# Weight parts at 32 places in turn, and the first layer's SwiGLU in three 256-column matmuls per weight tile

## The chip, the cores and the metric

The kernel runs on one core of a Trainium2 chip. A core has a matrix engine (TensorE, PE in the profile; its weight loads are listed apart as PEld), a vector engine (VectorE, DVE), a scalar engine (ScalarE, ACT), GpSimd (POOL) and a queue engine (SyncE, SP) that issues transfers. They share an on-chip memory of 128 partitions (SBUF); TensorE writes its results into banks of a second one (PSUM), from which the vector and scalar engines read. Each engine has its own instruction stream, and the streams wait for one another through semaphores.

The metric is the device time of one execution, in microseconds; lower is better.

## What is computed

Two layers of a decoder trunk over 256 positions and 1024 channels, in float32. The parts that matter here, cut from the reference:

```python
D_MODEL, SEQ, DEPTH, D_FF = 1024, 256, 2, 2816

def swiglu(h, w_in, w_out):
    a, b = jnp.split(h @ w_in, 2, axis=-1)
    return (jax.nn.silu(a) * b) @ w_out

for l in range(DEPTH):
    x = x + 0.5 * swiglu(rmsnorm(x, ffn1_norm[l]), ffn1_w_in[l], ffn1_w_out[l])
    h = rmsnorm(x, mix_norm[l])
    hq, hf, hi, hg, aq, ak, av, ga, gb = jnp.split(h @ w_in[l], split_idx, axis=-1)
    ...   # a gated recurrence and a dilated attention, merged by two gates
    x = x + merged @ w_out[l]
    x = x + 0.5 * swiglu(rmsnorm(x, ffn2_norm[l]), ffn2_w_in[l], ffn2_w_out[l])
```

All weights are read once, some 250 MB, and every product is a matrix of 256 positions against a weight matrix.

## The kernel before, in words

**Split operands.** A float32 product is made of three products of type float32r. Each operand is split in two parts: `hi`, the value rounded to that type, and `lo`, the rest. The product is hi·hi + hi·lo + lo·hi. Weights are split on the chip: `unit` (L200 on) starts a transfer of up to 1024 x 256 weights into a tile `raw` on SP's queue, then takes two `weight_parts` tiles of 4 x 128 rows each; ACT copies `raw` into `hi` (L211), DVE subtracts to get `lo` (L212). `raw` has three buffers and the tile of the parts, `wp`, four. The activations are kept split as well, feature-major: `xp` (the normed input of a stage), `hp` (the hidden values of a SwiGLU), `pp` and `obp` (in the mixer).

**Where the parts lie.** `weight_parts(at, c)` (L96) makes a tile of 8,704 bytes per partition, and puts `hi` at byte `at` and `lo` 4,096 bytes behind it; 512 bytes are spare. `unit` asks for `at` = 0 and `wide` for 32. In the program as built, the four `wp` tiles begin at bytes 83,680, 92,384, 101,088 and 109,792 of the partition, all 96 past a multiple of 128. So the parts of `unit` begin 96 past a multiple of 128 and those of `wide` on a multiple of 128. `xp`, `hp`, `pp` and `obp` all begin on multiples of 128.

**Three ways to multiply.** A weight tile here is 128 rows by 128 columns.

- `mm_pair` (L230 on) takes two matmuls for one: `hi` weights against both activation parts side by side, 512 columns (L237), and `lo` weights against the activation's `hi` part, 256 columns (L238), added into the second half of the same bank. Each block of 128 outputs has a bank of its own, and its two halves are added afterwards by `total` (L267): ACT copies one half out (L269), DVE adds the other (L270).
- `mm_feat` (L216 on) takes three matmuls of 256 columns (L226, L227, L228), all into the same 256 columns of a bank. Two blocks of 128 outputs share one bank and nothing is added afterwards.
- `wide` (L272 on, matmuls at L247 to L249) turns it round: the activations are the stationary side, and `wp` is streamed, 512 columns at a time, three matmuls each.

Each matmul loads its stationary operand itself, so there are as many weight loads as matmuls.

**Stages.** For each layer: a SwiGLU (`ffn`, L335 on), the mixer (`mix`), a second SwiGLU. A SwiGLU first runs over 11 blocks of 256 hidden columns; a block takes two units, `pa` and `pb`, each summed by `total`, multiplied by the norm's scale `Rb2` (L351, L356), passed through Silu, multiplied, and split into `hp`. Then it runs over four blocks of 256 outputs, each from three units over the 22 blocks of hidden rows, and adds half of the result into `xT` (L389, four instructions a block). All SwiGLU products use `mm_pair`, but for the last output product of the second layer, which uses `wide`. The mixer uses `mm_feat` (through `full`) and `wide`.

PSUM has eight banks: four for these products (`ps_mm`), three for small ones, one for transposes. A planner orders the instructions of each engine when the program is built.

Of the kernel before, what the change touches and what calls it, by code (L numbers as in the profile page):

```python
# [1 line left out]

# [1 line left out]

# [5 lines left out]
F32 = mybir.dt.float32  # L10
# [3 lines left out]
OP = mybir.AluOpType  # L14
# [5 lines left out]
DFF = 2816  # L20
KF = DFF // 128
CU = 256
# [5 lines left out]
FIRST = 2  # L28
# [49 lines left out]
def trunk(ctx, tc, x, ffn1_norm, ffn1_w_in, ffn1_w_out, mix_norm, w_in, lb_logits, out_norm,  # L78
          q_norm, k_norm, w_a, w_b, w_out, ffn2_norm, ffn2_w_in, ffn2_w_out, ctab, out):
    nc = tc.nc  # L80
# [4 lines left out]
    ps_mm = ctx.enter_context(tc.tile_pool(name="ps_mm", bufs=MM, space=PSUM))  # L85
    ps_sm = ctx.enter_context(tc.tile_pool(name="ps_sm", bufs=SM, space=PSUM))

    def bank(tag="sm"):
        return ps_sm.tile([128, 512], F32, name=tag, tag=tag, bufs=SM if tag == "sm" else 8 - MM - SM)

    def parts_of(pool, n, name, at=STEP, pad=STEP):

        t = pool.tile([128, n * 2 * T + pad // 4], F32R, name=name, bufs=1)
        return t[:, at // 4:at // 4 + n * 2 * T].rearrange("p (k a t) -> p k a t", a=2, t=T)

    def weight_parts(at, c):  # L96


        n = KH * CU
        t = wts.tile([128, 2 * n + LINE // 4], F32R, name="wp", bufs=WB)  # L100
        return [t[:, at // 4 + i * n:at // 4 + (i + 1) * n].rearrange("p (k c) -> p k c", c=c) for i in range(2)]

    def halves(p):
        return p[:, :, 0, :], p[:, :, 1, :]


    xT = const.tile([128, KD, T], F32, name="xT")
    xp = parts_of(const, KD, "xp", 128, LINE)
    xh, xl = halves(xp)
    ct = const.tile([128, C_END], F32, name="ct")  # L110
# [89 lines left out]
    def unit(w, r0, nk, col, step=0):  # L200
        raw = wts.tile([128, KD, CU], F32, name="raw", bufs=RB)
        for a in range(0, nk, step or nk):
            n = min(step or nk, nk - a)
            nc.sync.dma_start(raw[:, a:a + n, :], w[r0 + a * 128:r0 + (a + n) * 128, col:col + CU].rearrange(
                "(k p) c -> p k c", p=128))
        parts = []
        for a in range(0, nk, step or KH):
            n = min(step or KH, nk - a)
            hi, lo = weight_parts(0, CU)
            r = raw[:, a:a + n, :]  # L210
            nc.scalar.activation(hi[:, :n, :], r, AF.Copy)  # L211
            nc.vector.tensor_sub(lo[:, :n, :], r, hi[:, :n, :].bitcast(F32))  # L212
            parts += [(hi[:, k, :], lo[:, k, :]) for k in range(n)]
        return parts
# [15 lines left out]
    def mm_pair(ps, wu, ap, k0, nk, first, last):  # L230

        for k in range(nk):
            hi, lo = wu[k]
            s, e = first and k == 0, last and k == nk - 1
            for fb in range(2):
                f = slice(fb * 128, (fb + 1) * 128)
                nc.tensor.matmul(ps[fb], hi[:, f], ap[:, k0 + k], start=s, stop=False, skip_group_check=True)  # L237
                nc.tensor.matmul(ps[fb][:, 1, :], lo[:, f], ap[:, k0 + k, 0, :], start=False, stop=e,  # L238
                                 skip_group_check=True)
# [17 lines left out]
    def bank_pair():  # L257
        return [ps_mm.tile([128, 2, T], F32, name="mm") for _ in range(2)]

    def full_pair(w, col, ap, step=0):  # L260

        wu = unit(w, 0, KD, col, step)
        ps = bank_pair()
        mm_pair(ps, wu, ap, 0, KD, True, True)
        return ps

    def total(dst, ps):  # L267
        for fb in range(2):
            nc.scalar.activation(dst[:, fb, :], ps[fb][:, 1, :], AF.Copy)  # L269
            nc.vector.tensor_add(dst[:, fb, :], ps[fb][:, 0, :], dst[:, fb, :])  # L270
# [20 lines left out]
    def v2(a):  # L291
        return a.rearrange("p (a b) -> p a b", a=2)


    def norm_parts(gi, l):
        for k in range(KD):
            nc.scalar.activation(xh[:, k, :], xT[:, k, :], AF.Copy, scale=gain(gi, l, k))
            nc.vector.scalar_tensor_tensor(xl[:, k, :], xT[:, k, :], gain(gi, l, k),  # L298
                                           xh[:, k, :].bitcast(F32), op0=OP.mult, op1=OP.subtract)
# [16 lines left out]
    def square_sums_x(work, x0):  # L316
        ss = work.tile([128, 2], F32, name="nss", bufs=1)
        sq = work.tile([128, 4, D // 4], F32, name="nsx", bufs=1)
        for h in range(2):
            nc.scalar.activation(sq, x0[:, :, h, :], AF.Square, accum_out=ss[:, h:h + 1])  # L320
        return ss

    def norm_scale(work, ss):
        ms = work.tile([128, 2], F32, name="nms", bufs=1)
        nc.vector.tensor_scalar(ms, ss, 1.0 / D, EPS, op0=OP.mult, op1=OP.add)
        nc.gpsimd.tensor_tensor(rstd, ms, mhalf[:, 0:2], op=OP.pow)
        pr = bank("tr")
        for h in range(2):
            nc.tensor.transpose(pr[:, h * 128:(h + 1) * 128], rstd[:, h:h + 1].to_broadcast([128, 128]), ident)
        nc.vector.tensor_copy(Rb, pr[:, :T])  # L330

    Rb2 = Rb[:, None, :].to_broadcast([128, 2, T])


    def ffn(l, gi, w1, w2, to_out, x0=None):  # L335
        norm_parts(gi, l)
        with ExitStack() as es:
            fp = es.enter_context(tc.tile_pool(name="ffn", bufs=2))
            hp = parts_of(fp, KF, "hp")
            hh, hl = halves(hp)  # L340
            xt = None
            for j in range(DFF // CU):
                pa = full_pair(w1, j * CU, xp, step=0 if j or l or gi else FIRST)
                if j == 0:
                    with tc.tile_pool(name="norm", bufs=2) as work:
                        norm_scale(work, square_sums(work) if x0 is None else square_sums_x(work, x0))
                if j == 1 and l == 0 and gi == 0:
                    load_tables()
                a = fp.tile([128, 2, T], F32, name="fa")
                total(a, pa)  # L350
                nc.vector.tensor_mul(a, a, Rb2)  # L351
                nc.scalar.activation(a, a, AF.Silu)
                pb = full_pair(w1, DFF + j * CU, xp)
                b = fp.tile([128, 2, T], F32, name="fb")
                total(b, pb)
                nc.vector.tensor_mul(b, b, Rb2)  # L356
                nc.vector.tensor_mul(a, a, b)
                s = slice(2 * j, 2 * j + 2)
                nc.scalar.activation(hh[:, s, :], a, AF.Copy)
                nc.vector.tensor_sub(hl[:, s, :], a, hh[:, s, :].bitcast(F32))  # L360
            if to_out:
                xt = fp.tile([128, 2, D], F32, name="xt", bufs=1)
                for h in range(2):
                    for q in range(2):
                        p = bank()
                        for j in range(4):
                            nc.tensor.transpose(p[:, j * 128:(j + 1) * 128],
                                                xT[:, 4 * q + j, h * 128:(h + 1) * 128], ident)
                        nc.vector.tensor_copy(xt[:, h, q * 512:(q + 1) * 512], p)
            if to_out:  # L370
                for c in range(D // CW):
                    ps = wide(w2, c * CW, hp, KF)
                    for h in range(2):
                        y = fp.tile([128, CW], F32, name="fy", bufs=2)
                        nc.vector.scalar_tensor_tensor(y, ps[h], 0.5, xt[:, h, c * CW:(c + 1) * CW],
                                                       op0=OP.mult, op1=OP.add)
                        nc.sync.dma_start(out[0, h * 128:(h + 1) * 128, c * CW:(c + 1) * CW], y)
            else:
                for c in range(D // CU):
                    ps = bank_pair()  # L380
                    k0 = 0
                    for nk in (8, 8, 6):
                        wu = unit(w2, k0 * 128, nk, c * CU)
                        mm_pair(ps, wu, hp, k0, nk, k0 == 0, k0 + nk == KF)
                        k0 += nk
                    for fb in range(2):
                        xs = xT[:, 2 * c + fb, :]
                        for a in range(2):
                            nc.vector.scalar_tensor_tensor(xs, ps[fb][:, a, :], 0.5, xs, op0=OP.mult, op1=OP.add)  # L389
# [387 lines left out]
```

## Time and profile before

| what | value |
|---|---|
| median of two runs | 1431.3 us (1431.08 and 1431.51) |
| the profiled execution, its own time | 1430.89 us |
| its span, first to last instruction | 1428.8 us |
| DVE busy, whole span | 1059.1 us (74%) |
| ACT busy, whole span | 842.7 us (59%) |
| POOL busy, whole span | 93.1 us (7%) |
| transfers | 252.95 MB, mean 177 GB/s, the main queue's packets 54.1% of the 16 engines' span |
| matmuls, weight loads | 9,426 each |

The span is the time between the first and the last instruction of the program; 2.1 us of the execution lie around it. The profile has one line for each engine with its busy time, the span in 40 slices, the chain of work that ended last, and groups of instructions by line and operation. Matmuls are pipelined, so the duration of one (some 280 or 390 ns) says little. What says how fast TensorE goes is the distance from one start to the next, which the timeline or the first and last start of a group give.

### The profile page before, as it was taken

The page shows a single profiled execution, that of the slowest core. Times are in us where ns is not written, and L with a number is a line of the kernel's source. Part 1 is how long each engine was busy: PE and PEld are TensorE (multiplying, and loading weights), DVE is VectorE, ACT ScalarE, POOL GpSimd, SP SyncE. Part 2 cuts the span into 40 slices and gives each one's busy share as a digit, 9 for nine tenths or more (in the row PEclk, how much of TensorE's full clock was granted, in tenths as well). Part 3 has the DMA queues.
Part 4 walks back from the last instruction along what each step waited for, and adds up shares of the span by engine and source line. Part 5 has one row for each costly group of instructions (what it writes and reads, how often), then busy time and mean ns, then how long its engine had stood idle before and what let it go on. Part 6 is the DMA issues. An engine that isn't in the chain of part 4 may idle for free.

```text
span 1428.8 us, 23520 instructions
## 1 busy us (share of the span) xinstructions
PE 1419.3 (99%) x9426; PEld 1267.5 (89%) x9426; DVE 1059.1 (74%) x1664; ACT 842.7 (59%) x1435; POOL 93.1 (7%) x86
## 2 busy tenths in 40 slices
PE   8999999999999999999999999999999999999998
PEld 7888898998889998888888888988988899988887
DVE  6877569876976587786577866798779766787763
ACT  6655447657864566565455554666577646565542
POOL 0000010002510000000000000100035000000000
PEclk9999999999999999999999999999999999999999
DMA  8655564445554365555656556544454534556553
GB/s 293 202 183 193 185 198 156 149 148 177 177 177 148 119 200 184 192 191 182 201 178 196 187 178 197 186 157 142 154 182 165 195 116 144 195 187 197 177 191 104
DMA packets 215869, 252.95 MB, mean 177 GB/s; under 512 B 4224, under 2 KB 182608, under 8 KB 215760
## 3 DMA queue, kind: packets, MB, share of 16 engines
q1 hardware_dynamic: 215584, 251.38, 54.1%
q8 instruction: 74, 1.21, 0.4%
q14 instruction: 35, 0.29, 0.1%
q10 hardware_dynamic: 176, 0.07, 0.0%
HBM read 250.39 MB, written 1.05 MB: 176 GB/s over the span
## 4 chain that ended last, share of the span: by engine, by line
PE 99%; DMA 0%; DVE 0%; SPq 0%; issue 0%
PE mm L237 31%; PE mm L238 16%; PE mm L247 8%; PE mm L249 8%; PE mm L248 8%; PE mm L226 7%; PE mm L228 7%; PE mm L227 7%; PE sm L462 1%; PE sm L642 1%; PE tr L621 1%; PE sm L661 1%; PE sm L653 1%; PE sm L663 0%; DMA x<-in_x_dram 0%; PE sm L527 0%
## 5 line engine op out<-in xcount | busy, mean ns | idle before, releaser
L212 DVE TENSOR_TENSOR wp<-raw,wp 128x1024 fp32r<-128x1024 f32 (+1 forms) x354 | 423.6, 1198 | 170.9 <-ACT wp L211 169.0
L211 ACT ACTIVATE wp<-raw 128x1024 fp32r<-128x1024 f32 (+1 forms) x354 | 367.1, 1038 | 278.5 <-PE mm L238 119.8
L237 PE MATMUL mm<-xp,wp 128*128 128x512 f32 x1408 | 490.5, 392 | 1.5 <-DVE xp L298 1.5
L238 PE MATMUL mm<-xp,wp 128*128 128x256 f32 x1408 | 396.9, 283 | 0.0
L237 PEld LDWEIGHTS mm<-xp,wp 128*128 128x128 f32 x1408 | 264.7, 189 | 56.6 <-ACT wp L211 1.9
L238 PEld LDWEIGHTS mm<-xp,wp 128*128 128x128 f32 x1408 | 267.1, 190 | 0.9 <-DVE wp L212 0.2
L285 DVE TENSOR_TENSOR wp<-raw,wp 128x1024 fp32r<-128x1024 f32 x126 | 155.8, 1237 | 58.2 <-ACT wp L284 57.9
L237 PE MATMUL mm<-hp,wp 128*128 128x512 f32 x528 | 183.2, 390 | 0.0
L284 ACT ACTIVATE wp<-raw 128x1024 fp32r<-128x1024 f32 x126 | 133.1, 1063 | 79.6 <-PE mm L249 43.7
L247 PE MATMUL mm<-wp,xp 128*128 128x512 f32 x416 | 164.7, 396 | 0.0
L249 PE MATMUL mm<-wp,xp 128*128 128x512 f32 x416 | 163.5, 393 | 0.0
L248 PE MATMUL mm<-wp,xp 128*128 128x512 f32 x416 | 162.8, 391 | 0.0
L238 PE MATMUL mm<-hp,wp 128*128 128x256 f32 x528 | 148.9, 282 | 0.0
L226 PE MATMUL mm<-xp,wp 128*128 128x256 f32 x512 | 144.4, 283 | 0.0
L228 PE MATMUL mm<-xp,wp 128*128 128x256 f32 x512 | 144.3, 282 | 0.0
L227 PE MATMUL mm<-xp,wp 128*128 128x256 f32 x512 | 143.9, 282 | 0.0
L237 PEld LDWEIGHTS mm<-hp,wp 128*128 128x128 f32 x528 | 99.1, 188 | 20.8
L238 PEld LDWEIGHTS mm<-hp,wp 128*128 128x128 f32 x528 | 99.8, 189 | 0.0
L226 PEld LDWEIGHTS mm<-xp,wp 128*128 128x128 f32 x512 | 96.1, 188 | 1.2 <-issue 0.2
L228 PEld LDWEIGHTS mm<-xp,wp 128*128 128x128 f32 x512 | 96.3, 188 | 0.7 <-issue 0.2
L227 PEld LDWEIGHTS mm<-xp,wp 128*128 128x128 f32 x512 | 96.1, 188 | 0.7
L249 PEld LDWEIGHTS mm<-wp,xp 128*128 128x128 f32 x416 | 78.1, 188 | 16.1
(200 smaller groups left out, 2044.0 us busy)
## 6 DMA issues: line engine op xcount, KB each, us to landing
raw<-in_ffn_w_in_dram SPq DMA_DIRECT2D x87, 1024.0 KB, 5.1
raw<-in_w_in_dram SPq DMA_DIRECT2D x84, 1024.0 KB, 5.1
raw<-in_ffn_w_out_dram SPq DMA_DIRECT2D x34, 1024.0 KB, 5.2
raw<-in_ffn_w_out_dram SPq DMA_DIRECT2D x12, 768.0 KB, 4.5
raw<-in_w_branch_a_dram SPq DMA_DIRECT2D x8, 1024.0 KB, 5.2
raw<-in_w_out_dram SPq DMA_DIRECT2D x8, 1024.0 KB, 5.9
raw<-in_w_branch_b_dram SPq DMA_DIRECT2D x8, 512.0 KB, 3.4
x<-in_x_dram SPq DMA_DIRECT2D x4, 256.0 KB, 4.5
```

The lines of the kernel that those rows point to most:

```text
L211: nc.scalar.activation(hi[:, :n, :], r, AF.Copy)
L212: nc.vector.tensor_sub(lo[:, :n, :], r, hi[:, :n, :].bitcast(F32))
L226: nc.tensor.matmul(o, hi[:, f], ah, start=s, stop=False, skip_group_check=True)
L227: nc.tensor.matmul(o, hi[:, f], al, start=False, stop=False, skip_group_check=True)
L228: nc.tensor.matmul(o, lo[:, f], ah, start=False, stop=e, skip_group_check=True)
L237: nc.tensor.matmul(ps[fb], hi[:, f], ap[:, k0 + k], start=s, stop=False, skip_group_check=True)
L238: nc.tensor.matmul(ps[fb][:, 1, :], lo[:, f], ap[:, k0 + k, 0, :], start=False, stop=e, skip_group_check=True)
L247: nc.tensor.matmul(o, ah[:, k0 + k, t], hi, start=s, stop=False, skip_group_check=True)
L248: nc.tensor.matmul(o, ah[:, k0 + k, t], lo, start=False, stop=False, skip_group_check=True)
L249: nc.tensor.matmul(o, al[:, k0 + k, t], hi, start=False, stop=e, skip_group_check=True)
L284: nc.scalar.activation(hi, r, AF.Copy)
L285: nc.vector.tensor_sub(lo, r, hi.bitcast(F32))
```

## The change

Two things are changed.

First, `weight_parts` adds to `at` a number that changes at each call: 4 x (11 n mod 32) bytes for the n-th call. As 11 and 32 have no common factor, 32 calls in a row take all 32 multiples of four bytes from 0 to 124 once. The 480 calls of the program take each of them 15 times. It holds for `unit` and `wide` alike, in both layers.

Second, in the first layer (`l` = 0) both SwiGLUs use `full` and `mm_feat` in place of `full_pair` and `mm_pair`, in the input product and the output product. `total` goes there: DVE multiplies the bank by `Rb2` directly. The output block is added to `xT` in one instruction of 512 columns where there were four of 256. The second layer keeps its two matmuls per weight tile.

```diff
+from itertools import count
...
+    places = count()
+
...
         n = KH * CU
+        at += 4 * (11 * next(places) % 32)
         t = wts.tile([128, 2 * n + LINE // 4], F32R, name="wp", bufs=WB)
...
+            part = full_pair if l else full
+
+            def scaled(dst, ps):
+                if l:
+                    total(dst, ps)
+                    ps = None
+                nc.vector.tensor_mul(dst, dst if ps is None else v2(ps), Rb2)
+
             for j in range(DFF // CU):
-                pa = full_pair(w1, j * CU, xp, step=0 if j or l or gi else FIRST)
+                pa = part(w1, j * CU, xp, step=0 if j or l or gi else FIRST)
...
-                total(a, pa)
-                nc.vector.tensor_mul(a, a, Rb2)
+                scaled(a, pa)
                 nc.scalar.activation(a, a, AF.Silu)
-                pb = full_pair(w1, DFF + j * CU, xp)
+                pb = part(w1, DFF + j * CU, xp)
                 b = fp.tile([128, 2, T], F32, name="fb")
-                total(b, pb)
-                nc.vector.tensor_mul(b, b, Rb2)
+                scaled(b, pb)
...
-                    ps = bank_pair()
+                    ps = bank_pair() if l else ps_mm.tile([128, 512], F32, name="mm")
...
-                        mm_pair(ps, wu, hp, k0, nk, k0 == 0, k0 + nk == KF)
+                        (mm_pair if l else mm_feat)(ps, wu, hp, k0, nk, k0 == 0, k0 + nk == KF)
                         k0 += nk
+                    if not l:
+                        xs = xT[:, 2 * c:2 * c + 2, :]
+                        nc.vector.scalar_tensor_tensor(xs, v2(ps), 0.5, xs, op0=OP.mult, op1=OP.add)
+                        continue
```

## The prediction

> **What bounds the kernel now.** I read the page first: its busy line, its clock line, then the chain that ended last.
>
> ```profile
> span 1428.8 us, 23520 instructions
> PE 1419.3 (99%) x9426; PEld 1267.5 (89%) x9426; DVE 1059.1 (74%) x1664; ACT 842.7 (59%) x1435; POOL 93.1 (7%) x86
> PEclk9999999999999999999999999999999999999999
> PE 99%; DMA 0%; DVE 0%; SPq 0%; issue 0%
> ```
>
> PE is the chain for 99% of the span, at the full granted clock. So the time is the number of matmuls times the distance between their starts; what other engines gain or lose is worth nothing unless it makes PE wait. The counts come from the view of groups by line and shape:
>
> ```profile
> L237 PE MATMUL mm<-xp,wp 128*128 128x512 f32 x1408 | 490.5, 392 | 1.5 <-DVE xp L298 1.5
> L237 PE MATMUL mm<-hp,wp 128*128 128x512 f32 x528 | 183.2, 390 | 0.0
> L226 PE MATMUL mm<-xp,wp 128*128 128x256 f32 x512 | 144.4, 283 | 0.0
> L226 PE MATMUL mm<-pp,wp 128*128 128x256 f32 x256 | 70.8, 280 | 0.0
> L226 PE MATMUL mm<-obp,wp 128*128 128x256 f32 x64 | 18.1, 283 | 0.0
> L247 PE MATMUL mm<-wp,xp 128*128 128x512 f32 x416 | 164.7, 396 | 0.0
> L247 PE MATMUL mm<-wp,hp 128*128 128x512 f32 x88 | 34.4, 390 | 0.0
> ```
>
> One row is one matmul for each weight tile (or `wide` group). So 1408 + 528 = 1936 tiles take two matmuls, 512 + 256 + 64 = 832 take three, and 416 + 88 = 504 `wide` groups take three. In all 2 x 1936 + 3 x 832 + 3 x 504 = 7,880 matmuls use `wp`. The mean durations, 280 to 396 ns, overlap; the pace is read from starts. These are the answers for single lines in undisturbed stretches (count, durations, first and last start), and pieces of the timeline:
>
> ```profile
> L237 PE MATMUL mm<-hp,wp x176: 390/390/390, 656.8 to 717.5; 128*128 128x512 f32 x176
> L237 PEld LDWEIGHTS mm<-xp,wp x1: 188/188/188, 717.7 to 717.7; 128*128 128x128 f32 x1
> L226 PE MATMUL mm<-xp,wp x15: 277/278/281, 323.5 to 328.4; 128*128 128x256 f32 x15
> L226 PE MATMUL mm<-pp,wp x62: 278/280/281, 512.1 to 533.7; 128*128 128x256 f32 x62
> L247 PE MATMUL mm<-wp,xp x22: 389/389/389, 339.8 to 354.1; 128*128 128x512 f32 x22
> 21.63 0.39 PE L237 MATMUL mm<-xp,wp 128*128 128x512 f32 x1
> 21.86 0.28 PE L238 MATMUL mm<-xp,wp 128*128 128x256 f32 x1
> 21.98 0.39 PE L237 MATMUL mm<-xp,wp 128*128 128x512 f32 x1
> ```
>
> Two matmuls a tile: (717.5 - 656.8) / 175 = 0.347 us; the same 0.35 us from 21.63 to 21.98 with `xp`. Three matmuls a tile: (328.4 - 323.5) / 14 = 0.350 us in one stretch, (533.7 - 512.1) / 61 = 0.354 us in another. A `wide` group: (354.1 - 339.8) / 21 = 0.681 us, 0.227 us a matmul. Starts are printed to 0.1 us, so I work with 347, 350 to 354 and 681 ns.
>
> **The change, part by part.**
>
> *Three matmuls for two.* Layer 0 has half of the four input products and two of the three output products that use pairs: 1408 / 2 + 528 x 2 / 3 = 704 + 352 = 1,056 weight tiles. Each goes from 347 ns to between 350 and 354 ns: 1,056 x 3 ns = 3.2 us to 1,056 x 7 ns = 7.4 us, all on the path, with 1,056 more matmuls and weight loads. Both values occur with the same tiles, so nothing tells which will hold; I take the middle, 5.3 us.
>
> A page would price this otherwise. The Trainium skill ("TensorE: Matmul & The Clock Gate", section "Back-to-back issue gap") gives columns / 2.4 plus 2.5 ns for a warm matmul; by it the third matmul would cost an estimated 2.5 ns a tile, 2.6 us in all. The rows go against the rule's level (it gives 325 ns for a pair where the trace has 347), so the rows decide.
>
> *The sums that go.* DVE and ACT lose work in layer 0. The prices are these groups:
>
> ```profile
> L269 ACT ACTIVATE fb<-mm 128x256 f32<-128x256 f32 x88 | 32.0, 385 | 49.3 <-PE mm L238 49.2
> L270 DVE TENSOR_TENSOR fb<-mm,fb 128x256 f32<-128x256 f32 x88 | 33.8, 422 | 16.9 <-ACT fb L269 16.8
> L351 DVE TENSOR_TENSOR fa<-fa,Rb 128x512 f32<-128x512 f32 x44 | 30.4, 691 | 1.2
> L707 DVE TENSOR_TENSOR mg<-mm,Rb 128x512 f32<-128x512 f32 x8 | 5.5, 691 | 3.0 <-PE mm L228 2.6
> L389 DVE SCALAR_TENSOR_TENSOR xT<-mm,xT 128x256 f32<-128x256 f32 x48 | 19.1, 418 | 17.2 <-PE mm L238 17.2
> L544 DVE SCALAR_TENSOR_TENSOR hgs<-mm,rstd,hgs 128x512 f32<-128x512 f32 x8 | 6.0, 746 | 0.1
> 534.00:657.00 123.00, 123.00 (x713) 109.03 (x713) 96.85 (x135) 73.98 (x112) 0.70 (x1) 1.00 0.58 189
> 657.00:718.00 61.00, 61.00 (x353) 54.08 (x353) 36.23 (x49) 28.85 (x36) 0.00 (x0) 1.00 0.57 187
> ```
>
> Layer 0 has 44 parts, each with two copies and two adds: ACT loses 88 x 0.385 = 34 us, DVE 88 x 0.42 = 37 us. The multiply by `Rb2` now reads the bank and waits for PE itself; the gate's multiply L707 does just that and takes the 691 ns that L351 takes from the other memory. Eight output blocks replace 4 x 0.418 = 1.67 us by one instruction of about the 0.746 us of L544. None of it is on the path: the last two rows (the stretch, then busy PE, PEld, DVE, ACT, POOL, then clock, share and rate of transfers) show PE busy for all of both stages of the second SwiGLU, with DVE at 97 of 123 us and 36 of 61. I put it at nothing. Nor is a stage's end worth anything: the last `hp` pair starts at 717.5 and the next stage's weight load at 717.7, as its first columns of `xT` were ready long before. No transfer, queue or wait is moved; each part holds one bank rather than two of four.
>
> *The places.* With the third matmuls, 7,880 + 1,056 = 8,936 will use `wp`: it is the stationary side of 7,424 and the streamed side of 1,512 (`wide`). Of 32 places, 28 are not multiples of 32 bytes, 16 are odd words. The trace shows multiples of 32 alone: stationary parts 96 past a multiple of 128 (`unit`) and on one (`xp` in `wide`), both at 0.227 to 0.23 us per 512 columns, so at that step the place costs nothing. Below it, PE's reading isn't shown. The writers' is: these instructions touch single words 16 bytes apart (first rows) or runs of four words and longer:
>
> ```profile
> L454 ACT ACTIVATE X<-W x8: 1151/1166/1177, 222.5 to 1005.3; 128x512 f32<-128x512 f32 x8
> L454 ACT ACTIVATE hqq<-X x8: 616/626/634, 226.8 to 1012.6; 128x512 f32<-128x512 f32 x8
> L212 DVE TENSOR_TENSOR wp<-raw,wp 128x1024 fp32r<-128x1024 f32 x338 | 412.7, 1222 | 162.9 <-ACT wp L211 161.4
> L285 DVE TENSOR_TENSOR wp<-raw,wp 128x1024 fp32r<-128x1024 f32 x126 | 155.8, 1237 | 58.2 <-ACT wp L284 57.9
> ```
>
> Single words 16 bytes apart cost ACT (1166 - 626) / 512 = 1.05 ns each more than runs of four. A part that begins off a 16-byte line has at most two such words, some 2 ns of DVE's 1,222, and DVE waits 163 us before L212 in all, so the writers are covered. (Places 0 and 32 differ by 15 ns in the last two rows, which lie in different stages.)
>
> For PE I bound a toll t per matmul from both sides. The nearest row to a toll is the clock's ramp at the start, where TensorE ran at half pace:
>
> ```profile
> 11.72 0.63 PE L237 MATMUL mm<-xp,wp 128*128 128x512 f32 x1
> 12.15 0.41 PE L238 MATMUL mm<-xp,wp 128*128 128x256 f32 x1
> 12.37 0.63 PE L237 MATMUL mm<-xp,wp 128*128 128x512 f32 x1
> ```
>
> A pair takes 0.65 us there, the 512 columns 0.43. Half of 0.65 is 0.325, so at full pace a pair carries 347 - 325 = 22 ns beyond streaming, 11 ns a matmul: a standing toll that appears only when TensorE reads twice as fast. The bounds: t = -11 ns (the toll vanishes off the present places) to +200 ns (a streamed operand at odd words falls back to the half pace, 0.43 for 0.23 us). I take 0: over all places the trace does show, stationary and streamed, at two of them each or more, the pace doesn't move.
>
> *Sum.* The profiled execution's 1430.89 us (span 1428.8 and 2.1 around it) + 5.3 = 1436.2. It lies 0.4 us under the median, so against the median it is 1431.3 + 5.3 = 1436.6; I say 1437.
>
> **The rivals.**
>
> *A second toll at odd words (slower).* PE takes its operands at a rate that leaves no slack at full clock, as the standing 11 ns say, and an operand that begins on an odd word costs the toll once more. Half of the 8,936 matmuls would carry it: 4,468 x 11 ns = 49 us, 1437 + 49 = 1486. It passes 2% (28.6 us; about what a measurement of this kernel can tell from no change) when all matmuls together average (28.6 - 5.3) / 8,936 = 2.6 ns. For it: the toll depends on the pace of reading. Against: the place has no effect at steps of 32 bytes. Its far end is the half pace for `wide` at odd words, 756 x 200 ns = 151 us, 1588.
>
> *The toll goes (faster).* If the 11 ns come from stationary and streamed parts that begin at places related by multiples of 32 bytes, half of the places lose it: 4,468 x 11 ns = 49 us, 1437 - 49 = 1388. It passes 2% at (28.6 + 5.3) / 8,936 = 3.8 ns a matmul. Against: the relation of the two places differs between `unit` (96) and `wide` (0 past a multiple of 128) with one pace, and the toll vanishes at half clock with the places unchanged.
>
> *A line more (no change, but later).* A row of weights, 512 bytes, that begins off a 16-byte line touches 33 lines for 32, and at the 16 odd places single words lie at an end. With ACT's 1.05 ns for such a word, on the 8,056 matmuls of the kernel after that have no slack for it (1,888 tiles x 3, 880 pairs' 256 columns, 1,512 of `wide`), half of them: 4,028 x 1.05 ns = 4.2 us, 1441. The L454 rows are for it, that they are ACT's and not PE's against. The Trainium skill has this rule ("SBUF — State Buffer", section "Specifications (TRN2)"): lines of 16 bytes, at least two hits on each for full rate, and a penalty at each crossing to a new one; the L454 rows agree, and no run here shows it on PE.
>
> *Nothing at all.* If three matmuls went at the pair's 347 ns, 1431. Every undisturbed stretch of L226 speaks against it.
>
> **How the numbers follow.** The forecast, places free and three matmuls at 350 to 354 ns (1434 to 1439): 0.58. A line more, 1441: 0.14. Nothing, 1431: 0.04. The second toll: 0.18, of which 0.02 stays below 2%. The toll goes: 0.06. So faster 0.06, same 0.58 + 0.14 + 0.04 + 0.02 = 0.78, slower 0.16. For 8 in 10, the range takes the forecast, the line, nothing, and the lower part of the second toll (to 3.7 ns a matmul on average: 33 us, 1470): 1429 to 1470. The forecast's own range is 1434 to 1439.
>
> **What would show it.** Right: in layer 0's SwiGLUs three starts per tile in 350 to 354 ns, in layer 1 pairs still 347 and `wide` still 681 while the places run; PE at 99%. The distance between starts, taken tile by tile, must not repeat with 32 `wp` tiles. Wrong: a pace that swings with the `wp` tile, in L247 to L249 alone if the streamed side is at fault, in all if the stationary side is; or DVE's subtraction far over 1,222 ns with PE waiting for it.

## The result, and the profile after

| | before | after |
|---|---|---|
| median | 1431.3 us (1431.08 to 1431.51) | 1452.11 us (1451.47 to 1452.74) |
| ratio | 1 | 1.0145, 95% interval 1.0102 to 1.0189 |
| span of the profiled execution | 1428.8 us | 1451.0 us |

The change makes the kernel 1.45% slower, 20.8 us. The forecast was 1437, the range 1429 to 1470.

These are the page's lines of the changed kernel that answer to those shown of before: span, busy time, granted clock, the chain, and the group of DVE's subtraction. The last line below is the same group on the page of before.

```profile
span 1451.0 us, 25413 instructions
PE 1441.0 (99%) x10482; PEld 1321.2 (91%) x10482; DVE 1027.3 (71%) x1552; ACT 818.0 (56%) x1347; POOL 91.1 (6%) x86
PEclk9999999999999999999999999999999999999999
PE 99%; DMA 0%; ACT 0%; SPq 0%; DVE 0%; issue 0%; ACTq 0%
L216 DVE TENSOR_TENSOR wp<-raw,wp 128x1024 fp32r<-128x1024 f32 (+1 forms) x354 | 424.4, 1200 | 213.8 <-ACT wp L215 212.1
```
```profile
L212 DVE TENSOR_TENSOR wp<-raw,wp 128x1024 fp32r<-128x1024 f32 (+1 forms) x354 | 423.6, 1198 | 170.9 <-ACT wp L211 169.0
```

TensorE is still the chain for 99%, at full clock, with 1,056 matmuls more. DVE lost 32 us of work and ACT 25, and nothing came of it. DVE's subtraction, 1198 ns on the page of before, takes 1200 (this group mixes two shapes; the larger alone, the prediction's 1222, takes 1224): the writers of the parts do not mind the places. PE's busy time grew by 21.7 us and the span by 22.2, so the change is in the distance between starts of matmuls. Here are four starts of L230 (the first of three matmuls on a tile) in two parts of the first stage, from the timeline of the changed kernel; the columns are start, duration, engine and line:

```profile
34.44 0.28 PE L230 MATMUL mm<-xp,wp 128*128 128x256 f32 x1
34.80 0.28 PE L230 MATMUL mm<-xp,wp 128*128 128x256 f32 x1
...
57.22 0.28 PE L230 MATMUL mm<-xp,wp 128*128 128x256 f32 x1
57.55 0.28 PE L230 MATMUL mm<-xp,wp 128*128 128x256 f32 x1
```

The first part lies at place 3 (12 bytes on): 0.36 us a tile. The second lies at place 27 (108 bytes): 0.33 to 0.34. Both are products with `xp`, from the same one of the four `wp` buffers, at the same clock. The pace swings with the `wp` tile, which the prediction named as the sign that it is wrong. Next, single lines in whole stretches of the changed kernel: the layer 0 output product (three matmuls), the layer 1 output product (pairs), the attention's `wide` products; and the last of these before the change:

```profile
L230 PE MATMUL mm<-hp,wp x176: 274/281/296, 668.5 to 730.4; 128*128 128x256 f32 x176
L241 PE MATMUL mm<-hp,wp x176: 387/394/425, 854.7 to 916.1; 128*128 128x512 f32 x176
L251 PE MATMUL mm<-wp,xp x144: 387/395/581, 337.8 to 445.2; 128*128 128x512 f32 x144
```
```profile
L247 PE MATMUL mm<-wp,xp x144: 387/389/582, 331.6 to 437.0; 128*128 128x512 f32 x144
```

Three matmuls: (730.4 - 668.5) / 175 = 354 ns a tile. Pairs, which the change leaves as pairs: (916.1 - 854.7) / 175 = 351 ns, where they had 347. The 144 groups of `wide` take 107.4 us for 105.4, with the attention's small matmuls among them in both.

Taking every start of the two traces, and leaving out those distances into which small matmuls of other work fell, the means by the way of multiplying are (in ns; the number is that of tiles or groups):

```
                              before   after   number    difference
layer 0, pair -> three        346.4    354.6   1056       8.7 us
mixer, three                  351.7    354.7    832       2.5 us
layer 1, pair                 346.3    350.0    880       3.3 us
wide, groups                  682.6    698.8    504       8.2 us
sum                                                      22.7 us
```

That is the 22.2 us of the span within 0.5. By place (means in ns, in the changed kernel; a place is 4 bytes):

```
place    0   1   2   3   4   5   6   7   8   9  10  11  12  13  14  15
three  351 360 354 359 356 358 353 360 359 354 348 351 356 359 359 352
wide   688 715 704 688 693 710 701 683 702 705 703 691 697 709 694 682
place   16  17  18  19  20  21  22  23  24  25  26  27  28  29  30  31
three  355 360 358 354 353 343 352 360 348 355 355 343 356 359 349 357
wide   687 720 704 686 693 712 709 694 700 719 695 684 691 717 701 692
```

Pairs lie between 347 and 353 ns at most places. The pattern mostly comes back when the place comes round, but a mean can hide two paces: of place 24's nine visits by three-matmul tiles, five have means of 342 to 344 ns and four of 350 to 353. For three matmuls two places, 21 and 27, are clearly better than the old one (place 0), three (10, 24 and 30) are 2 to 3 ns better, and most are worse; for `wide` none is better than the fixed byte 32 (682), and those 4 bytes past a multiple of 16 (1, 5, 9 and so on) are the worst group.

### The profile page after: what moved, and what is told of

It is laid out like the page before. It is cut to its first block, busy times and chain, and to the rows that moved or that the text cites. A ratio compares the mean times of both kernels' runs of the same rounds, so it can differ in the third digit from the quotient of the medians.

```text
span 1451.0 us, 25413 instructions
## 1 busy us (share of the span) xinstructions
PE 1441.0 (99%) x10482; PEld 1321.2 (91%) x10482; DVE 1027.3 (71%) x1552; ACT 818.0 (56%) x1347; POOL 91.1 (6%) x86
## 4 chain that ended last, share of the span: by engine, by line
PE 99%; DMA 0%; ACT 0%; SPq 0%; DVE 0%; issue 0%; ACTq 0%
PE mm L230 16%; PE mm L232 16%; PE mm L231 16%; PE mm L241 14%; PE mm L251 8%; PE mm L253 8%; PE mm L252 8%; PE mm L242 7%; PE sm L476 1%; PE sm L656 1%; PE tr L635 1%; PE sm L675 1%; PE sm L667 1%; DMA x<-in_x_dram 0%; PE sm L677 0%; PE sm L541 0%
## 5 line engine op out<-in xcount | busy, mean ns | idle before, releaser
L230 PE MATMUL mm<-xp,wp 128*128 128x256 f32 x1216 | 343.6, 283 | 1.4 <-ACT wp L215 1.4
L232 PE MATMUL mm<-xp,wp 128*128 128x256 f32 x1216 | 343.7, 283 | 0.0
L231 PE MATMUL mm<-xp,wp 128*128 128x256 f32 x1216 | 343.3, 283 | 0.0
L241 PE MATMUL mm<-xp,wp 128*128 128x512 f32 x704 | 246.8, 395 | 0.0
L230 PEld LDWEIGHTS mm<-xp,wp 128*128 128x128 f32 x1216 | 229.8, 189 | 3.1 <-ACT wp L215 1.8
L232 PEld LDWEIGHTS mm<-xp,wp 128*128 128x128 f32 x1216 | 230.0, 189 | 0.9 <-DVE wp L216 0.2
L231 PEld LDWEIGHTS mm<-xp,wp 128*128 128x128 f32 x1216 | 229.9, 189 | 0.6
L242 PE MATMUL mm<-xp,wp 128*128 128x256 f32 x704 | 197.2, 281 | 0.0
L251 PE MATMUL mm<-wp,xp 128*128 128x512 f32 x416 | 166.8, 401 | 0.0
L253 PE MATMUL mm<-wp,xp 128*128 128x512 f32 x416 | 165.4, 398 | 0.0
L252 PE MATMUL mm<-wp,xp 128*128 128x512 f32 x416 | 164.7, 396 | 0.0
L241 PEld LDWEIGHTS mm<-xp,wp 128*128 128x128 f32 x704 | 132.1, 188 | 30.5
L242 PEld LDWEIGHTS mm<-xp,wp 128*128 128x128 f32 x704 | 132.5, 188 | 0.3
L231 PE MATMUL mm<-hp,wp 128*128 128x256 f32 x352 | 98.7, 281 | 0.0
L230 PE MATMUL mm<-hp,wp 128*128 128x256 f32 x352 | 98.7, 280 | 0.0
L232 PE MATMUL mm<-hp,wp 128*128 128x256 f32 x352 | 98.7, 280 | 0.0
L253 PEld LDWEIGHTS mm<-wp,xp 128*128 128x128 f32 x416 | 78.4, 189 | 17.8
L252 PEld LDWEIGHTS mm<-wp,xp 128*128 128x128 f32 x416 | 78.6, 189 | 16.9
```

Of the source, the lines that this page charges most:

```text
L230: nc.tensor.matmul(o, hi[:, f], ah, start=s, stop=False, skip_group_check=True)
L231: nc.tensor.matmul(o, hi[:, f], al, start=False, stop=False, skip_group_check=True)
L232: nc.tensor.matmul(o, lo[:, f], ah, start=False, stop=e, skip_group_check=True)
L251: nc.tensor.matmul(o, ah[:, k0 + k, t], hi, start=s, stop=False, skip_group_check=True)
L252: nc.tensor.matmul(o, ah[:, k0 + k, t], lo, start=False, stop=False, skip_group_check=True)
L253: nc.tensor.matmul(o, al[:, k0 + k, t], hi, start=False, stop=e, skip_group_check=True)
```

## The experiments

The theory after this reading: two costs that add, the third matmul (about 5 us) and the places (about 17), of which the streamed and the stationary side each pay a part, and each place has a pace of its own. Ratios are to the kernel before, run on the same chip; it had 1430.3 to 1430.6 us in the three sets of runs, so times of different sets can be compared.

**e1, the third matmul alone.** The changed kernel without its first part:

```diff
-        at += 4 * (11 * next(places) % 32)
```

> The second part of the change alone: layer 0's SwiGLUs in three matmuls per weight tile, every weight part at its old place. Theory (two costs that add: the third matmul, and the places): layer 0's 1,056 tiles go from the 346.4 ns between starts that the trace of before has for pairs to the 351.7 ns that it has for its three-matmul tiles, 5.6 us, so 1437, ratio 1.004. Rival (the third matmul is dear by itself, the places are harmless): most of the 20.8 us, 1448 to 1452.

Measured: 1434.41 us, ratio 1.0029 (1.0018 to 1.0039), 3.9 us over before. The layer 0 output product in its trace, by the line of the first matmul:

```profile
L229 PE MATMUL mm<-hp,wp x172: 277/279/281, 138.1 to 197.9; 128*128 128x256 f32 x172
```

(197.9 - 138.1) / 171 = 350 ns, the lower of the two paces that the prediction had. The third matmul is the small part.

**e2, the places alone.** The kernel before with the first part only:

```diff
+        at += 4 * (11 * next(places) % 32)
```

> The first part of the change alone: the 32 places, in both layers, with two matmuls per weight tile in all SwiGLUs but the last output product. Theory (the costs add): by the distances between starts of the changed kernel's trace, pairs take 350.0 for 346.4 ns (1,936 tiles, 7.0 us), three-matmul tiles of the mixer 354.5 for 351.7 (832, 2.3 us), groups of wide 699 for 682.3 (504, 8.4 us): 17.7 us, 1449, ratio 1.012. Rival (the places harm only where three loads share a tile): about 1433 to 1435.

Measured: 1447.9 us, ratio 1.0117 (1.0102 to 1.0133). Layer 0's output product, in pairs:

```profile
L241 PE MATMUL mm<-hp,wp x174: 387/393/403, 137.3 to 197.8; 128*128 128x512 f32 x174
```

(197.8 - 137.3) / 173 = 350 ns where pairs had 347. The rival falls: pairs suffer without any new three-matmul tile, and so does `wide`. 3.9 us of e1 and 17.4 us of e2 make 21.3, each over before, against 20.8 for both together: the two costs add, as far as the 20.8 can tell (it rests on two runs of each kernel, with an interval of 15 to 27 us).

**e3, the places on the stationary side alone.**

```diff
-        at += 4 * (11 * next(places) % 32)
+        at += 4 * (11 * next(places) % 32) if c == CU else 0
```

> The changed kernel, but wide's parts, which TensorE streams, stay at byte 32; the parts of unit, which it holds stationary, keep the 32 places. Theory (both sides pay, the streamed side about half of it): 504 groups of wide go back from 699 to 682.3 ns, 8.4 us less, 1452 - 8.4 = 1443.7. Rival (what costs is a change of place from one part to the next, on either side): wide's groups stay above 682.3 at the borders, a time over 1446.

Measured: 1444.41 us, ratio 1.0095 (1.0078 to 1.0112), near the 1443.7 expected. Groups of `wide` are back at a mean of 682.6 ns. Over before, e3 has 13.9 us, the whole change 20.8 and e1 3.9: so the streamed side's places cost 6.9 us, the stationary side's 10.0, the third matmul 3.9. The split is rough: the table of means has 8.2 us for `wide`.

**e4, one good place.** All parts of `unit` at place 21:

```diff
-        at += 4 * (11 * next(places) % 32)
+        at += 84 if c == CU else 0
```

> The changed kernel, but every part of unit begins at place 21 (byte 84) and wide's at byte 32. At place 21 the changed kernel's trace has 343 ns for a three-matmul tile, 340 in the steady part, and 353 for a pair; place 21 fell always on the same one of the four wp buffers. Theory (the place alone sets the pace): 1,888 three-matmul tiles at 341.5 ns, so layer 0 gains 1,056 x 4.9 = 5.2 us on before and the mixer 832 x 10.2 = 8.5, layer 1's 880 pairs lose 6.5 ns each, 5.7 us: 1431.3 - 8 = 1423. Rival (it was the buffer, or the change of place before it): three-matmul tiles at 351 to 355 on average, 1437 to 1445.

Measured: 1428.34 us, ratio 0.9984 (0.9974 to 0.9993), under the kernel before. Layer 0's output product in three matmuls, then layer 1's in pairs:

```profile
L230 PE MATMUL mm<-hp,wp x173: 276/276/276, 133.8 to 192.3; 128*128 128x256 f32 x173
...
L241 PE MATMUL mm<-hp,wp x154: 396/398/399, 835.8 to 889.9; 128*128 128x512 f32 x154
```

(192.3 - 133.8) / 172 = 340 ns for three matmuls, less than the 347 of a pair at its old place, on all four `wp` buffers; (889.9 - 835.8) / 153 = 354 for pairs. The place is a cause, whatever the buffer, and what is good for one way of multiplying is bad for the other. The time is 5 us above the expected 1423: the mixer's 832 tiles came to a mean of 349.5 ns, not 341.5, which is 6.7 us.

**e5, activations moved rather than weights.** The kernel of e1, with

```diff
-    xp = parts_of(const, KD, "xp", 128, LINE)
+    xp = parts_of(const, KD, "xp", 44, LINE)
...
-            hp = parts_of(fp, KF, "hp")
+            hp = parts_of(fp, KF, "hp", 76, 96)
```

and `pp` and `obp` alike.

> Weight parts all at their old places (the kernel of e1), but the streamed activations moved: xp begins 84 bytes earlier, hp, pp and obp 44 bytes past a multiple of 128. The distance from streamed to stationary operand is then what place 21 gave. Theory (the distance between the two operands sets the pace): three-matmul tiles near 340 ns in the SwiGLUs as in e4, pairs 353, about 1426 to 1428. Rival A (the stationary operand's own address sets it): three-matmul tiles stay at 351, pairs at 346.5, 1434. Rival B (the streamed operand's own start sets it too): neither pattern; every tile slower by a like amount.

Measured: 1449.31 us, ratio 1.0132 (1.0117 to 1.0147). None of the three: layer 0's output product in three matmuls, layer 1's in pairs, and a stretch of `wide`, for which the activations are the stationary side:

```profile
L229 PE MATMUL mm<-hp,wp x165: 279/279/279, 139.8 to 197.7; 128*128 128x256 f32 x165
L240 PE MATMUL mm<-hp,wp x146: 389/389/391, 853.0 to 902.9; 128*128 128x512 f32 x146
L250 PE MATMUL mm<-wp,xp x28: 400/400/400, 345.0 to 364.1; 128*128 128x512 f32 x28
```

(197.7 - 139.8) / 164 = 353 ns where the distance theory wanted 340, (902.9 - 853.0) / 145 = 344 where it wanted 353, and (364.1 - 345.0) / 27 = 707 for the 682 of e1. The distance between the operands does not set the pace alone, nor does the weights' address alone. (The 353 of three matmuls would not exclude the distance by itself, as e8 finds that pace at place 21 too; the pairs and the time do.)

**e6, activations 4 bytes on.** The kernel of e1 with `xp` at 132, and `hp`, `pp` and `obp` 4 bytes past a multiple of 128.

```diff
-    xp = parts_of(const, KD, "xp", 128, LINE)
+    xp = parts_of(const, KD, "xp", 132, LINE)
```

> Weight parts all at their old places (the kernel of e1), the streamed activations xp, hp, pp and obp 4 bytes further. Theory of e5 (distance): this is place 31 of the changed kernel, three-matmul tiles 356.9 for 350.9 ns and pairs 349.6 for 346.5: 1,888 x 6 + 880 x 3.1 ns = 14 us over e1, 1448. Rival A (stationary address alone): 1434. Rival B (a streamed operand that begins 4 bytes past a 16-byte line is dear, as wide's groups show with 715 for 680 ns, 11 ns on each 512 columns): 17 ns a tile, 1,888 + 880 tiles, 46 us, 1480.

Measured: 1471.64 us, ratio 1.0287 (1.027 to 1.0305). Three matmuls:

```profile
L229 PE MATMUL mm<-hp,wp x166: 280/284/289, 143.0 to 202.9; 128*128 128x256 f32 x166
```

(202.9 - 143.0) / 165 = 363 ns for 350, 4.3 ns a matmul, and pairs go to a mean of 356. Rival B is nearest (1480), with a smaller price than that of `wide`. No weight part moved here: the activations' start costs 37 us over e1, more than the whole change. Not all of it is the streamed side, because `wide` holds the activations stationary:

```profile
L250 PE MATMUL mm<-wp,xp x30: 388/392/399, 344.7 to 364.9; 128*128 128x512 f32 x30
```

(364.9 - 344.7) / 29 = 697 ns for the 679 of e1 (shown under e7); over 504 groups that is an estimated 9 us, which leaves some 28 us, still more than the whole change, for the streamed side.

**e7, `wide` at byte 36.** The kernel of e1 with

```diff
-                hi, lo = weight_parts(STEP, CW)
+                hi, lo = weight_parts(STEP + 4, CW)
```

> The kernel of e1 with one thing changed: wide's parts begin at byte 36, not 32, all of them. Theory (the streamed operand's place alone costs): groups of wide at 714.6 ns as at place 1 of the changed kernel, for 682.4: 504 x 32 ns = 16 us over e1, 1450. Rival (the cost comes from places that differ between parts in a row): groups stay near 682, 1434 to 1437.

Measured: 1448.6 us, ratio 1.0128 (1.0113 to 1.0143). A stretch of e7, then the same of e1:

```profile
L250 PE MATMUL mm<-wp,xp x29: 394/401/403, 339.7 to 359.7; 128*128 128x512 f32 x29
```
```profile
L250 PE MATMUL mm<-wp,xp x30: 389/389/389, 339.7 to 359.4; 128*128 128x512 f32 x30
```

(359.7 - 339.7) / 28 = 714 ns for (359.4 - 339.7) / 29 = 679. Four bytes, the same for all parts, 14 us. The streamed side pays for the place, not for its changing.

**e8, three matmuls in both layers at place 21.** The kernel of e4 with

```diff
-            part = full_pair if l else full
+            part = full
```

and the sums of both layers as in layer 0.

> Three matmuls per weight tile in both layers' SwiGLUs, every part of unit at place 21 (byte 84), wide's at byte 32. Theory (place 21 suits three matmuls): layer 1's 880 tiles go from e4's 353 to 340 to 341 ns, 11 us under e4's 1428.3: 1417, ratio to before 0.991. Rival (place 21 keeps the fast pace only in a part of the stretches, as in the mixer's output product of e4 with 353): 1422 or more.

Measured: 1416.81 us, ratio 0.9906 (0.9891 to 0.992). The theory's number. But part of the rival is true as well; the mixer's output product, same place, same kind of tile:

```profile
L230 PE MATMUL mm<-pp,wp x60: 279/284/284, 507.8 to 528.6; 128*128 128x256 f32 x60
```

(528.6 - 507.8) / 59 = 353 ns, where `hp`, which in layer 0's second SwiGLU begins at the same byte as `pp`, goes at 340. So a place does not fix one pace. The old place shows it too: layer 0's SwiGLUs have the same addresses in e1 and e7, and the output product that went at 350 ns in e1 goes at 353 in e7, (198.5 - 137.0) / 174:

```profile
L229 PE MATMUL mm<-hp,wp x175: 278/278/278, 137.0 to 198.5; 128*128 128x256 f32 x175
```

These are the prediction's 350 and 354, which occurred with the same tiles. In these traces an undisturbed stretch keeps the pace it has.

**e9, a round place.** The kernel of e1 with all parts of `unit` 32 bytes on, at a multiple of 128:

```diff
+        at += 32 if c == CU else 0
```

> The kernel of e1 with every part of unit at place 8, byte 32, so that weights and activations all begin on multiples of 128 bytes. Theory (each place has its own pace, round addresses are not safe): three-matmul tiles at 359.2 ns as at place 8 of the changed kernel, for 350.9; pairs unchanged at 346.7: 1,888 x 8.3 ns = 16 us over e1, 1450. Rival (only starts off a 16-byte line cost, as in the prediction's line rival, and multiples of 32 bytes are alike, as its forecast took them to be): 1434.

Measured: 1454.39 us, ratio 1.0165 (1.0148 to 1.0182), 20 us over e1, and no faster than the change itself.

```profile
L230 PE MATMUL mm<-hp,wp x165: 283/283/283, 140.7 to 199.7; 128*128 128x256 f32 x165
```

(199.7 - 140.7) / 164 = 360 ns. Pairs were expected unchanged; they went to 350 to 353 in the mean, which makes the rest of the time over 1450.

**e10, place 27.** The kernel of e8 with 108 for 84.

```diff
-        at += 84 if c == CU else 0
+        at += 108 if c == CU else 0
```

> The kernel of e8 with place 27 (byte 108) for place 21. Theory (each place has its own pace): place 27 has 343.0 ns for a three-matmul tile in the changed kernel, like place 21's 343.2, 340 in the steady part, so the time of e8, 1417. Rival (the gain of e8 is of place 21 and its neighbours in time, not of a place): 1425 to 1432, with tiles at 347 or more.

Measured: 1410.43 us, ratio 0.9861 (0.9846 to 0.9876), better than expected. Its page and its layer 0 output product:

```profile
span 1408.8 us, 26973 instructions
PE 1398.5 (99%) x11362; PEld 1324.0 (94%) x11362; DVE 993.2 (70%) x1452; ACT 790.4 (56%) x1259; POOL 92.5 (7%) x86
```
```profile
L230 PE MATMUL mm<-hp,wp x174: 276/276/276, 133.0 to 191.8; 128*128 128x256 f32 x174
```

As many matmuls as e8 and e11, more than any other kernel here, and the least time: (191.8 - 133.0) / 173 = 340 ns, and here the mixer's tiles too go at 340 to 343 in most stretches. Not in all: two stretches with `pp`, at the same addresses, still differ.

```profile
L230 PE MATMUL mm<-pp,wp x16: 282/283/283, 455.3 to 460.7; 128*128 128x256 f32 x16
...
L230 PE MATMUL mm<-pp,wp x28: 276/276/276, 517.4 to 526.6; 128*128 128x256 f32 x28
```

(460.7 - 455.3) / 15 = 360 ns, then (526.6 - 517.4) / 27 = 341. This version beats both kernels, by 1.4% and by 2.9%.

**e11, places 21 and 27 in turn.** The kernel of e8 with

```diff
-        at += 84 if c == CU else 0
+        at += 84 + 24 * (next(places) % 2) if c == CU else 0
```

> The kernel of e8 with parts of unit at places 21 and 27 in turn, two places that are both fast. Theory (a place sets the steady pace and a change of place costs its first tiles: after a border the changed kernel's trace has some 354 and 349 ns at places 21 and 27 before 340): some 23 ns for each part of eight tiles, in the SwiGLUs 250 parts, 6 us over e8, 1423. Rival A (a change of place costs nothing): 1417. Rival B (the change is most of the cost of the 32 places, 16.8 us over all): 1430 or more.

Measured: 1411.32 us, ratio 0.9867 (0.9853 to 0.9882).

```profile
L230 PE MATMUL mm<-hp,wp x175: 276/276/276, 132.7 to 191.9; 128*128 128x256 f32 x175
```

(191.9 - 132.7) / 174 = 340 ns, through all borders. The expected 6 us did not come: going from one of these places to the other costs nothing. That the first tiles after a border are slow in the changed kernel may then come from the place before, from which the old pace is carried over; this was not tried apart.

## Why the prediction was right and wrong

- **The bound** was right: PE is 99% of the chain before and after, and every microsecond of the change lies in the distance between starts.
- **The third matmul** was right: 5.3 us predicted, between 3.2 and 7.4; e1 has 3.9, and 350 ns a tile is the lower of the two paces quoted.
- **The sums that go, the stages' ends, the writers**: at nothing, and rightly. DVE's subtraction kept its 1200 ns; DVE has 32 us less to do and ACT 25, somewhat less than the 37 and 34 priced from mean durations, and nothing of it shows in the time.
- **The places** were wrong. The step that failed is "at that step the place costs nothing", with which the toll was set to 0. Two places were compared, one of them for pairs and the other for `wide`, and what held for them was carried over to all tiles and to all places. The rows already held a warning: "0.227 to 0.23 us per 512 columns" fits pairs and `wide`, but three matmuls at 350 to 354 ns are 0.233 to 0.236, with two paces on the same tiles. e9 is the counterexample inside the step itself: a multiple of 32 bytes costs three-matmul tiles 10 ns, 3.3 ns a matmul. The toll is 17.4 us over e2's 7,880 matmuls, 2.2 ns each, or 16.9 us over 8,936 (the difference of the change and e1), 1.9 ns each: inside the bounds of -11 to 200 ns, and inside the range of times, which was made for it.
- **The forecast's own range**, 1434 to 1439, missed for that one term: 1437 would have been 1454 with it, against 1452.
- **"A second toll at odd words"** has the right sign, not the mechanism. Odd places 21 and 27 are the fastest for three matmuls and even place 8 is among the slowest (e9, e10). For a streamed operand the start within 16 bytes does count: 4 bytes past a multiple was slow wherever it was tried (e6, e7) and is the worst group in the table for `wide`.
- **"A line more"** is refuted for PE by e9: a start on a line is dear, starts off it (e4, e10) are cheap. The Trainium skill's rule of 16-byte lines ("SBUF — State Buffer", section "Specifications (TRN2)") agrees with ACT's rows in the prediction; no run here shows it as what sets the stationary side's pace.
- **"The toll goes"** was given 0.06, and as a forecast for this change it was wrong; but a part of the toll does go at two of the 32 places: three-matmul tiles fall from 351 to 340 ns, some 3.7 ns a matmul of the 11 that the prediction had, and e10 is made of that. Its reason is not borne out: pairs get slower at place 21 (e4), and the same distance between the operands gives no such gain in e5. The argument against it, that the pace was one at two distances between the operands, was the same step that failed.
- **The chances**: within 2% had 0.78 and came, slower by over 2% had 0.16. That it came is in part luck: of the 0.78 only 0.16 (a line more, and a small second toll) allowed for places that cost anything, and the average of 1.9 ns a matmul lies not far below the 2.6 at which the prediction passes 2%.

What stays open: the rule by which the two addresses give a pace. e5 and e6 exclude that it is the distance alone or the weights' address alone. Why the same place has two paces (e8, e10, and the old place in e1 and e7), and what chooses between them, is not settled either; that an undisturbed stretch keeps its pace was seen, not tried.

## What to carry to other kernels

When TensorE is the bound, the address of each operand is a tuning knob, worth 1 to 3% in this kernel, at steps of 4 bytes, for the stationary and the streamed side apart, and for each way of multiplying anew. A kernel that turns through all places is a cheap way to find good ones, since the trace has the pace of every one; it is not a kernel to keep, and a place that looks good has to be tried alone, because a pace can be carried over from the place before. And "two values agree" is evidence for the case in which they were compared, not for the parameter.

## What the runs showed of the hardware that was not expected

- Three matmuls of 256 columns on a weight tile can take less than one of 512 and one of 256 for the same columns: 340 ns at places 21 and 27, against 347 for the pair at its old place. The Trainium skill's gap for isolated warm matmuls ("TensorE: Matmul & The Clock Gate", section "Back-to-back issue gap") would be an estimated 327.5 ns for the three; no stretch of these tiles came under 340.
- Round addresses are no safe choice: with weights and activations both on multiples of 128 bytes, three-matmul tiles take 360 ns (e9), while `wide`, both of whose operands begin there in the kernel before, is at its best (682).
- Moving all activations by 4 bytes costs 37 us over e1, 2.6% (e6); moving the streamed weights of `wide` by 4 bytes takes its groups from 679 to 714 ns (e7).
- At one place two steady paces exist: 340 and 353 ns at place 21 (e8), 340 and 360 at place 27 (e10), 350 and 353 at the old place (e1 and e7).
